# Sample tokens' experts gathered on four partition groups, dense experts on 512 tokens, an exponential decay, and new row quotas in a hybrid trunk layer

## The chip, the cores and the metric

One core of one Trainium2 chip runs the whole kernel. The metric is the device time of one execution in microseconds (us), the median of the runs shown. All data are fp32 in HBM; the large matmuls are done in passes of a high and a low half, as told below.

## The reference, cut to what matters

One layer is computed for 1024 prompt tokens and 32 sample tokens (next frames of a running stream), with D = 1024 channels. Three mixers (a gated convolution, an RG-LRU recurrence, an HGRN2 matrix recurrence) read one wide projection of x and are merged, a layer norm follows, then PEER: each token takes 8 heads x 16 = 128 single-neuron experts out of 16384.

```python
log_a = -LRU_C * r * softplus(-lam)            # RG-LRU, r a sigmoid
a = exp(log_a)
u = sqrt(-expm1(2.0 * log_a)) * (gi * xf)
h_t = a_t * h_{t-1} + u_t

def peer_block(xt, wq, keys, u_tab, v_tab):    # u_tab, v_tab: 16384 x 1024
    q = (xt @ wq).reshape(n, 8, 2, 128)
    s = einsum('nhpd,hpkd->nhpk', q, keys)
    sv, si = top_k(s, 16)                      # per half, then 16 of the 256 pair sums
    ...
    h = gelu(einsum('nd,nhkd->nhk', xt, u_tab[expert]))
    return einsum('nhk,nhkd->nd', g * h, v_tab[expert])
x = layer_norm(ALPHA * x + merged @ w_o)
x = layer_norm(ALPHA * x + peer(x))
```

## The kernel before

The tokens are taken in two halves: tokens 0 to 511 (four tiles of 128), then tokens 512 to 1023 together with the 32 sample tokens. Activations lie with channels on partitions. Every projection (`proj`, lines 327 to 340) has a 128-column weight tile in a high part wh (cast by ScalarE, L293) and a low part wl (the difference, made by VectorE at L297, or read back from HBM at L295), and eight k tiles of the input, again as high and low; it issues wh*xh (L334), wh*xl (L335) and wl*xh (L339), so 24 passes over all columns of the layout. A layout `Lay(n)` of over 512 columns is cut in two halves, and then each pass is two matmuls; one of 512 is one matmul.

PEER is done in two ways. **Gathered**: the first four tiles (the list `todo`, tokens 0 to 511). `gather` (L1214) loads, for each of a token's 128 experts, one row of `u` per partition by an indirect DMA that GpSimd issues (L1221; one "row" is a 128 x 1024 fp32 tile, 512 KB), multiplies and sums it on VectorE (L1230), then gelu, then the same with rows of `v` (L1238), and a layer norm. That is 256 rows per tile, 1024 in all, and they go through four row buffers (`big`, L878): GpSimd issues row k+4 when VectorE has used row k. **Dense**: tokens 512 to 1023 and the 32 sample tokens, 544 columns in two halves of 272. All 16384 experts' activations are computed as 128 projections of `ut` (`hidden`, L1091; 40 of them ahead of time, in the spread stage, kept in HBM as `hd`), multiplied by a weight matrix `gt` that is zero but for the chosen experts (L1134), cut in high and low (L1138, L1139), and multiplied by `vt` in 16 groups of 8 projections (L1146), added into eight accumulators (L1152). The weight matrix is made by `spread`, for 16 tokens at a time, from one-hot products (L1080, L1083, L1084) and staged in HBM as `gd`, 34 blocks of 16 tokens.

The rows of the gathered tiles are traced last in the program, and the framework's scheduler fixes each engine's order ahead of time; VectorE then runs its list strictly in order. `BESIDE` and `pacing` (L1256) hold the rows back: the program has marks (`cuts`) between stages, `BESIDE` says how many rows belong to each stage, and a row's VectorE instruction may not stand before an instruction at the matching share of that stage's matmuls. It is a lower bound only: nothing makes a row stand there if its data, its buffer or VectorE is not free. The seven stages and quotas of before are:

- the rest of the first half's top-k with mixer A of the second half: 92
- heads of the second half (`heads`): 125
- `outs` of the second half (mixer C's output, mixer B): 145
- output of mixer B, first norm, top-k of the second half: 94
- spread: 42
- dense groups 0 to 4, whose hidden projections were done ahead: 82
- dense groups 5 to 15, with 8 hidden and 8 `vt` projections each: 444 (spread over 97% of the matmuls, `EARLY`)

Mixer B (`mix_b`, L566) has the recurrence. Its decay a = exp(-2x) is formed from t = tanh(x) as 1 - 2t/(1+t), with a reciprocal on VectorE (L611) and, in the second half, two ScalarE affine steps (L608, L614); sqrt(t)/(1+t) scales the input (L604, L619, L620). It is called eight times in each half.

Of the kernel before, what the change touches and what calls it, by code (L numbers as in the profile page):

```python
# [57 lines left out]
BESIDE = 92, 125, 145, 94, 42, 82, 444  # L58
# [4 lines left out]
SPAN = 39  # L63
# [38 lines left out]
class K:  # L102
# [51 lines left out]
    def consts(self):  # L154
# [28 lines left out]
        pi = c.tile([128, 1], I32, name="pi")  # L183
        G.iota(pi, pattern=[[0, 1]], base=0, channel_multiplier=1)
        ct = ExitStack()
        t = ct.enter_context(self.tc.tile_pool(name="ct", bufs=1))
        ti = t.tile([128, 128], I32, name="ti")
# [9 lines left out]
        pb = c.tile([128, 1], I32, name="mpb")  # L197
        pf = c.tile([128, 2], F32, name="mpf")
# [73 lines left out]
        V.scalar_tensor_tensor(self.sp2, p, 4.0, u, op0=OP.mult, op1=OP.add)  # L272

# [292 lines left out]
    def mix_b(self, ct, out):  # L566
# [31 lines left out]
        t = tr  # L598
# [442 lines left out]
    def experts(self, ti, ijg):  # L1041
        V, B = self.nc.vector, self.bp
        ex = B.tile([128, 128], I32, name="ex", tag=f"ex{ti}")
        V.scalar_tensor_tensor(ex, ijg[:, 0:128], 128.0, ijg[:, 128:256], op0=OP.mult, op1=OP.add)  # L1044
        gw = B.tile([128, 128], F32, name="gw", tag=f"gw{ti}")
        V.tensor_copy(gw, ijg[:, 256:384])
        return ex, gw


    def spread(self, n, c0, ijg, H):  # L1050
# [4 lines left out]
        if H == 8:  # L1055
            for q in range(3):
                nc.tensor.transpose(pt[:, q * 128:(q + 1) * 128], ijg[:, q * 128:(q + 1) * 128], self.ident)
# [348 lines left out]
```

## Time and profile before

| | us |
|---|---|
| median of three runs | 4102.07 (4100.8 to 4104.7) |
| the profiled execution | 4098.35 |
| its span, first to last instruction | 4096.2 |
| PE busy / VectorE busy / ScalarE busy / GpSimd busy | 3799.3 / 3205.3 / 1471.7 / 1528.8 |

All later terms are made against the profiled execution: its time is 2.2 us more than its span, and 3.7 us below the median of the runs. The page gives the busy time of each engine, and busy shares in 40 slices; a matmul's end is modelled, so a busy PE is not PE at its peak rate. The rows below take the span apart by the stages above. The stretches meet where one stage's own lines end and the next one's begin: 1547 us is the end of the heads, 1846 the last mixer B product (L634), 2220 the last copy of a query (L940), 2661 the start of the dense groups, 2946 the first hidden projection of dense group 5, 4066 the last accumulation.

### The profile page before, as it was taken

What the parts mean: (1) busy time and instruction counts of PE and PEld (TensorE: products, weight loads), DVE (VectorE), ACT (ScalarE), POOL (GpSimd) and SP (SyncE); (2) the same over time, 40 slices, a digit from 0 to 9 for tenths busy, and PEclk for the clock granted to TensorE, in tenths of its full rate; (3) what the DMA queues carried; (4) which work ended last, traced back from release to release, by engine and by line L of the source; (5) the groups of instructions that cost most, each with busy time, mean ns of one, the idle gap of its engine ahead of it and who ended that gap; (6) DMA issues with size and microseconds to landing.
All of it is one profiled execution on the core that took longest, in us unless ns stands there. A gap on an engine that the chain in (4) does not pass through costs nothing.

```text
span 4096.2 us, 69951 instructions
## 1 busy us (share of the span) xinstructions
PE 3799.3 (93%) x26917; PEld 3543.6 (87%) x26917; DVE 3205.3 (78%) x6625; ACT 1471.7 (36%) x2352; POOL 1528.8 (37%) x1353
## 2 busy tenths in 40 slices
PE   9999999989899898999678998789999999999996
PEld 7888787789899887999668997689999999999996
DVE  6556438679997887885689999888788887878888
ACT  3333326433232223552233588722222222222222
POOL 0000000001345543343332688723356555555553
PEclk9999999999999998999889999899999999999998
DMA  5443455668998977998997887798899988888886
GB/s 189 144 144 132 154 190 177 217 236 299 366 341 295 319 277 246 339 321 334 366 343 283 279 277 241 214 337 317 287 321 325 324 315 306 315 311 315 316 317 233
DMA packets 377230, 1132.94 MB, mean 277 GB/s; under 512 B 34816, under 2 KB 109696, under 8 KB 374848
## 3 DMA queue, kind: packets, MB, share of 16 engines
q1 hardware_dynamic: 229440, 591.53, 40.9%
q0 software_dynamic: 147456, 536.94, 37.4%
q8 instruction: 212, 3.47, 0.3%
q14 instruction: 122, 1.00, 0.1%
HBM read 1000.48 MB, written 127.84 MB: 275 GB/s over the span
## 4 chain that ended last, share of the span: by engine, by line
PE 16%; DMA 11%; issue 9%; DVE 7%; POOL 6%; ACT 2%; SPq 0%; POOLq 0%; DVEq 0%; ACTq 0%
DMA row<-in_v,ex 7%; POOL row L1221 6%; PE z L339 5%; PE z L335 5%; PE z L334 4%; DVE x1g L1238 2%; PE t L1084 1%; DMA row<-in_u,ex 1%; DVE oa L1080 1%; DMA wl<-wl 1%; DVE wl L297 1%; ACT stg L1085 1%; DMA wraw<-in_wq 1%; DMA ge<-hd 1%; ACT ob L1074 0%
## 5 line engine op out<-in xcount | busy, mean ns | idle before, releaser
L334 PE MATMUL z<-h,wh 128*128 128x272 f32 (+5 forms) x4608 | 1315.4, 313 | 30.4 <-ACT wh L293 18.0
L335 PE MATMUL z<-l,wh 128*128 128x272 f32 (+5 forms) x4608 | 1303.7, 310 | 1.2 <-DVE l L370 1.2
L1221 POOL DMA_INDIRECT row<-in_u,ex x512 | 628.0, 1227 | 1510.0 <-DVE ex L1044 655.8
L293 ACT CAST wh<-wraw 128x1024 fp32r<-128x1024 f32 x568 | 596.3, 1050 | 1414.1 <-PE z L335 1130.7
L334 PEld LDWEIGHTS z<-h,wh 128*128 128x128 f32 x4608 | 878.0, 191 | 77.1 <-ACT wh L293 21.5
L1221 POOL DMA_INDIRECT row<-in_v,ex x512 | 665.4, 1300 | 688.5 <-DVE x1g L1238 469.4
L335 PEld LDWEIGHTS z<-l,wh 128*128 128x128 f32 x4608 | 878.8, 191 | 37.4 <-issue 2.7
L339 PE MATMUL z<-h,wl 128*128 128x272 f32 (+5 forms) x4608 | 744.6, 309 | 14.9 <-DMA wl<-wl 14.2
L1238 DVE SCALAR_TENSOR_TENSOR x1g<-row,hh,x1g 128x1024 f32<-128x1024 f32 x512 | 655.1, 1280 | 125.4 <-DMA row<-in_v,ex 121.7
L1230 DVE SCALAR_TENSOR_TENSOR row<-row,x1g 128x1024 f32<-128x1024 f32 x512 | 618.2, 1217 | 145.0 <-DMA row<-in_u,ex 144.4
L339 PEld LDWEIGHTS z<-h,wl 128*128 128x128 f32 x4608 | 649.9, 190 | 49.6 <-DMA wl<-wl 15.5
L297 DVE TENSOR_TENSOR wl<-wraw,wh 128x1024 fp32r<-128x1024 f32 x400 | 488.5, 1222 | 187.4 <-ACT wh L293 89.7
L335 PE MATMUL z<-dl,wh 128*128 128x272 f32 x2048 | 518.1, 292 | 29.6 <-DVE dl L1139 29.4
L334 PE MATMUL z<-dh,wh 128*128 128x272 f32 x2048 | 515.3, 293 | 10.2 <-ACT dh L1138 9.8
L335 PEld LDWEIGHTS z<-dl,wh 128*128 128x128 f32 x2048 | 386.3, 192 | 35.1 <-DVE dl L1139 35.1
L334 PEld LDWEIGHTS z<-dh,wh 128*128 128x128 f32 x2048 | 384.6, 192 | 14.3 <-ACT dh L1138 14.2
L339 PE MATMUL z<-dh,wl 128*128 128x272 f32 x2048 | 283.9, 292 | 23.8 <-DVE wl L297 23.8
L339 PEld LDWEIGHTS z<-dh,wl 128*128 128x128 f32 x2048 | 269.8, 192 | 25.4 <-DVE wl L297 25.4
L1138 ACT CAST dh<-w 128x544 fp32r<-128x544 f32 x128 | 82.4, 647 | 393.1 <-DVE w L1134 393.1
L1083 POOL TENSOR_SCALAR ob<-iota,tr 128x128 f32<-128x128 f32 x272 | 214.3, 801 | 22.1 <-PE t L1084 8.7
L1084 PE MATMUL t<-ob,oa 128*128 128x128 f32 x1088 | 167.8, 293 | 33.6 <-DVE oa L1080 15.9
L1084 PEld LDWEIGHTS t<-ob,oa 128*128 128x128 f32 x1088 | 147.8, 199 | 47.5 <-POOL ob L1083 15.1
(381 smaller groups left out, 4650.4 us busy)
## 6 DMA issues: line engine op xcount, KB each, us to landing
wl<-wl SPq DMA_DIRECT2D x304, 512.0 KB, 4.7
wraw<-in_w_in SPq DMA_DIRECT2D x192, 512.0 KB, 4.3
wraw<-in_vt SPq DMA_DIRECT2D x128, 512.0 KB, 6.4
wraw<-in_ut SPq DMA_DIRECT2D x128, 512.0 KB, 5.8
gd<-stg SPq DMA_DIRECT2D x34, 1024.0 KB, 6.3
gt<-gd SPq DMA_DIRECT2D x16, 2176.0 KB, 11.5
wraw<-in_wq SPq DMA_DIRECT2D x56, 512.0 KB, 6.9
wraw<-in_w_o SPq DMA_DIRECT2D x24, 512.0 KB, 6.2
```

Source lines behind the costliest of these rows:

```text
L293: nc.scalar.copy(wh, raw)
L297: nc.vector.tensor_sub(wl, raw, wh.bitcast(F32))
L334: mm(ps[:, :n], wh[:, k, :], xh[:, o:o + n], start=k == 0, stop=False)
L335: mm(ps[:, :n], wh[:, k, :], xl[:, o:o + n], start=False, stop=False)
L339: mm(ps[:, :n], wl[:, k, :], xh[:, o:o + n], start=False, stop=k == KT - 1)
L1080: V.tensor_scalar(oa, self.iota, tr[:, 0, t:t + 1], tr[:, 2, t:t + 1], op0=OP.is_equal, op1=OP.mult)
L1083: G.tensor_scalar(ob, self.iota, tr[:, 1, t:t + 1], None, op0=OP.is_equal)
L1084: nc.tensor.matmul(pw[:, s * 128:(s + 1) * 128], oa, ob, start=True, stop=True)
L1138: A.copy(hi, w)
L1221: nc.gpsimd.indirect_dma_start(out=u[:n], out_offset=None, in_=self.io[tab], in_offset=bass.IndirectOffsetOnAxis(ap=ex[:n, s:s + 1], axis=0))
L1230: V.scalar_tensor_tensor(u[:n], u[:n], 1.0, x1[:n], op0=OP.mult, op1=OP.mult, accum_out=hh[:n, s:s + 1])
L1238: V.scalar_tensor_tensor(x1[:n], u[:n], hh[:n, s:s + 1], x1[:n], op0=OP.mult, op1=OP.add)
```

## The change

- The sample's 32 tokens leave the dense part. Their 128 experts are kept as a 128 x 32 block, as `retrieve` already makes it (two heads' 32 experts on each of four groups of 32 partitions). The new `gather_packed` copies x1 of the 32 tokens four times onto the partitions, runs 32 rows of u and 32 rows of v on all 128 partitions, adds the four groups by three small DMAs and adds, and normalizes. It is traced ahead of the last gathered tile. That makes 1088 rows in place of 1024.
- The dense part has 512 tokens: one matmul of 512 columns per pass. `spread` loses its sample case: 32 blocks of 16 tokens instead of 34. The final tail has four tiles.
- `mix_b` computes a = exp(-2 sp2 (tr + 1)) by one ScalarE activation and takes 0.5 (1 + a) sqrt(t) as the input's scale: the reciprocal and the affine steps go.
- `BESIDE` becomes 92, 125, 195, 140, 35, 50, 451, and `SPAN` 37.

```diff
-BESIDE = 92, 125, 145, 94, 42, 82, 444
+BESIDE = 92, 125, 195, 140, 35, 50, 451
-SPAN = 39
+SPAN = 37
...
+        self.sp4 = e8("sp4")
+        V.tensor_scalar(self.sp4, self.sp2, -2.0, None, op0=OP.mult)
...
-        t = tr
+        t, a = sq, tr
...
         A.activation(t[:, :N], tr[:, :N], AF.Tanh, scale=self.sp2[:, ct:ct + 1], bias=self.sp2[:, ct:ct + 1])
+        A.activation(a[:, :N], tr[:, :N], AF.Exp, scale=self.sp4[:, ct:ct + 1], bias=self.sp4[:, ct:ct + 1])
         A.activation(sq[:, :N], t[:, :N], AF.Sqrt)
-        rc, a = self.et(), t
-        if b and FA > 1:
-            A.activation(rc[:, :N], t[:, :N], AF.Identity, bias=self.one)
-        else:
-            V.tensor_scalar(rc[:, :N], t[:, :N], 1.0, None, op0=OP.add)
-        V.reciprocal(rc[:, :N], rc[:, :N])
-        V.tensor_mul(a[:, :N], t[:, :N], rc[:, :N])
-        if b and FA:
-            A.activation(a[:, :N], a[:, :N], AF.Identity, scale=-2.0, bias=self.one)
-        else:
-            V.tensor_scalar(a[:, :N], a[:, :N], -2.0, 1.0, op0=OP.mult, op1=OP.add)
...
-        V.tensor_mul(v[:, :N], v[:, :N], sq[:, :N])
-        V.tensor_mul(v[:, :N], v[:, :N], rc[:, :N])
+        V.scalar_tensor_tensor(sq[:, :N], a[:, :N], 1.0, sq[:, :N], op0=OP.add, op1=OP.mult)
+        V.scalar_tensor_tensor(v[:, :N], v[:, :N], 0.5, sq[:, :N], op0=OP.mult, op1=OP.mult)
...
+            if H < 8:
+                self.packed = (t, *self.experts(t[0], ijg))
             yield
-            yield from self.spread(t[3], t[2], ijg, H)
+            if H == 8:
+                yield from self.spread(t[2], ijg)
...
+    def gather_packed(self, t, ex, gw):
+        nc, (_, g0, _, n) = self.nc, t
+        V = nc.vector
+        x1 = self.x1g(128)
+        for q in range(4):
+            nc.sync.dma_start(x1[n * q:n * q + n], self.x1d[g0:g0 + n, :])
+        def mid():
+            V.tensor_scalar(x1[:n], x1[:n], ALPHA, None, op0=OP.mult)
+            for q in range(1, 4):
+                V.memset(x1[n * q:n * q + n], 0.0)
+        self.retrieved(x1, 128, ex, gw, 32, x1, mid)
+        for q in range(1, 4):
+            u = self.big()
+            nc.sync.dma_start(u[:n], x1[n * q:n * q + n])
+            V.tensor_add(x1[:n], x1[:n], u[:n])
+        self.finished(x1, g0, n)
...
-    k.gd = k.dp.tile([16, 128, 34, 128], F32, name="gd")
+    k.gd = k.dp.tile([16, 128, 32, 128], F32, name="gd")
-        dt = k.tiles(1)[4 - ND:]
+        dt = k.tiles(1)[4 - ND:4]
-            c0, L = (4 - ND) * 128, Lay(ND * 128 + SMP)
+            c0, L = (4 - ND) * 128, Lay(ND * 128)
         for t in todo:
+            if t is todo[-1]:
+                k.gather_packed(*k.packed)
-            k.gather(t[0], t[1], t[3], t[4], t[5])
+            k.gather(t[1], t[3], t[4], t[5])
```

`retrieved` and `rows`, which both gathers call, hold the loops of the old `gather` unchanged but for the number of rows.

## Rows read from the trace of the kernel before

**Rows 1.** The profile's page: span, busy time by engine, and the DMA engines' busy tenths in 40 slices of the span.

```profile
span 4096.2 us, 69951 instructions
PE 3799.3 (93%) x26917; PEld 3543.6 (87%) x26917; DVE 3205.3 (78%) x6625; ACT 1471.7 (36%) x2352; POOL 1528.8 (37%) x1353
...
DMA  5443455668998977998997887798899988888886
```

**Rows 2.** The busy times by stretch, all instructions: stretch, its length, busy us (and instructions) of PE, PEld, DVE, ACT, POOL, then granted clock, DMA share, GB/s.

```profile
700.00:800.00 100.00, 96.73 (x404) 75.10 (x403) 72.33 (x93) 52.12 (x67) 0.00 (x0) 1.00 0.58 201
...
1547.00:1846.00 299.00, 289.95 (x2147) 273.68 (x2148) 238.48 (x363) 151.56 (x224) 113.94 (x93) 0.97 0.85 307
...
2220.00:2661.00 441.00, 389.63 (x2971) 374.64 (x2971) 421.49 (x1237) 313.87 (x615) 320.08 (x354) 0.96 0.80 253
2661.00:2946.00 285.00, 260.30 (x1971) 255.53 (x1970) 225.12 (x350) 69.93 (x86) 86.58 (x80) 0.96 0.89 317
2946.00:4066.00 1120.00, 1080.65 (x8492) 1074.01 (x8490) 928.44 (x1185) 294.72 (x445) 608.90 (x442) 0.99 0.89 314
4066.00:4096.20 30.20, 0.00 (x0) 0.00 (x0) 25.43 (x53) 8.92 (x16) 0.00 (x0) 0.53 0.27 99
```

**Rows 3.** The same view for line 1221 alone, the row issues on GpSimd: stretch, its length, POOL busy (and issues), granted clock, DMA share, GB/s. The last row is the same view for line 1238 (rows of v used by VectorE), for one stretch of 100 us.

```profile
970.00:1150.00 180.00, 62.69 (x59) 1.00 0.96 360
1150.00:1547.00 397.00, 189.03 (x152) 0.94 0.86 303
1547.00:1846.00 299.00, 113.94 (x93) 0.97 0.85 307
1846.00:2220.00 374.00, 126.51 (x117) 0.88 0.91 338
2220.00:2661.00 441.00, 105.77 (x82) 0.96 0.80 253
2661.00:2946.00 285.00, 86.58 (x80) 0.96 0.89 317
2946.00:4066.00 1120.00, 608.90 (x442) 0.99 0.89 314
...
3100.00:3200.00 100.00, 55.09 (x43) 1.00 0.94 333
```

**Rows 4.** The timeline of PE inside dense group 12: start us, duration, line, operation. One projection of 48 matmuls of 272 columns lies between the first and the last row.

```profile
3760.62 0.29 PE L334 MATMUL z<-h,wh 128*128 128x272 f32 x1
...
3764.63 2.16 PE L339 MATMUL z<-h,wl 128*128 128x272 f32 x16
3766.63 0.29 PE L334 MATMUL z<-h,wh 128*128 128x272 f32 x1
```

**Rows 5.** The timeline of PE in the first half, where the layout has 512 columns: 16 matmuls start between these two rows.

```profile
212.49 0.39 PE L334 MATMUL z<-h,wh 128*128 128x512 f32 x1
...
216.21 2.02 PE L339 MATMUL z<-h,wl 128*128 128x512 f32 x8
```

**Rows 6.** VectorE's groups of instructions in the stretch 2946 to 4066 us: line, operation, tiles, shape, count | busy us, mean ns | idle us ahead of them and who ended it.

```profile
L1238 DVE SCALAR_TENSOR_TENSOR x1g<-row,hh,x1g 128x1024 f32<-128x1024 f32 x255 | 326.8, 1282 | 89.7 <-DMA row<-in_v,ex 87.0
L1230 DVE SCALAR_TENSOR_TENSOR row<-row,x1g 128x1024 f32<-128x1024 f32 x190 | 228.8, 1221 | 68.4 <-DMA row<-in_u,ex 67.9
...
L1152 DVE TENSOR_TENSOR acc<-acc,z 128x272 f32<-128x272 f32 x178 | 70.2, 430 | 28.1 <-PE z L339 27.8
L1139 DVE TENSOR_TENSOR dl<-w,dh 128x544 fp32r<-128x544 f32 x88 | 63.2, 718 | 0.0
...
L1230 DVE DVE_READ_ACCUMULATOR row<-row,x1g 128x1 f32 x190 | 15.4, 81 | 0.0
```

**Rows 7.** VectorE's waits in the same stretch: who waited for whom, us in total, times, longest.

```profile
DVE x1g L1238 <- DMA row<-in_v,ex: 87.0, 68, 6.1
DVE row L1230 <- DMA row<-in_u,ex: 67.9, 50, 6.9
```

**Rows 8.** PE's longest waits in the same stretch.

```profile
PE z L339 <- DVE wl L297: 23.8, 7, 4.4
```

**Rows 9.** Row DMAs in the same stretch: issues, and median us from issue to landing.

```profile
row<-in_v,ex POOLq DMA_INDIRECT x256, 6.8
row<-in_u,ex POOLq DMA_INDIRECT x186, 6.5
```

**Rows 10.** Groups of instructions of mixer B, whole span: two of VectorE in the second half, and ScalarE's table loads ahead of the square root (L604) and of the gelu (L589).

```profile
L611 DVE RECIPROCAL e<-e 128x548 f32<-128x548 f32 x8 | 28.6, 3575 | 1.1 <-ACT e L608 1.1
...
L612 DVE TENSOR_TENSOR e<-e 128x548 f32<-128x548 f32 x8 | 5.8, 723 | 0.0
...
L604 ACT ACT_TABLE_LOAD x16 | 20.5, 1283 | 0.3
L589 ACT ACT_TABLE_LOAD x14 | 18.0, 1283 | 0.2
```

**Rows 11.** VectorE's costliest group in the spread stage, 2220 to 2661 us.

```profile
L1080 DVE TENSOR_SCALAR oa<-iota,tr 128x128 f32<-128x128 f32 x544 | 170.7, 393 | 0.0
```

**Rows 12.** Two VectorE groups on 512 columns in the first half, one with an operand in PSUM (L854) and one without (L634).

```profile
L854 DVE SCALAR_TENSOR_TENSOR m<-e,z 128x512 f32<-128x512 f32 x8 | 5.5, 685 | 22.4 <-PE z L339 22.4
...
L634 DVE TENSOR_TENSOR e<-e 128x512 f32<-128x512 f32 x8 | 5.5, 682 | 0.0
```

**Rows 13.** The timeline of GpSimd where the third gathered tile ends and the fourth begins: in brackets the idle time ahead of the issue and who ended it.

```profile
3423.56 1.68 POOL L1221 DMA_INDIRECT row<-in_u,ex  x1 [8.06 <-DVE x1g L874]
```

More of the change, by code (lines that the diff above doesn't have):

```diff
@@ L196, in consts @@
         tb = t.tile([128, 128], I32, name="mtb")
-        pb = c.tile([128, 1], I32, name="mpb")
-        pf = c.tile([128, 2], F32, name="mpf")
+        pb = t.tile([128, 1], I32, name="mpb")
+        pf = t.tile([128, 2], F32, name="mpf")
         tf = t.tile([128, 128], F32, name="mtf")
@@ L1042, in experts, with spread @@
         V, B = self.nc.vector, self.bp
[L1043 to L1046, printed above, removed]
+        m = ijg.shape[1] // 3
+        ex = B.tile([128, m], I32, name="ex", tag=f"ex{ti}")
+        V.scalar_tensor_tensor(ex, ijg[:, 0:m], 128.0, ijg[:, m:2 * m], op0=OP.mult, op1=OP.add)
+        gw = B.tile([128, m], F32, name="gw", tag=f"gw{ti}")
+        V.tensor_copy(gw, ijg[:, 2 * m:3 * m])
         return ex, gw
-    def spread(self, n, c0, ijg, H):
+    def spread(self, c0, ijg):
         nc = self.nc
@@ L1211, in paced @@
         return self.tc.issue_after(self.pace[min(k, len(self.pace) - 1)])
-    def gather(self, ti, g0, n, ex, gw):
-        nc = self.nc
-        V, A, B = nc.vector, nc.scalar, self.gp
-        hh = B.tile([128, 128], F32, name="hh", tag="hh", bufs=2)
-        def row(tab, s):
-            u = self.big()
-            nc.gpsimd.indirect_dma_start(out=u[:n], out_offset=None, in_=self.io[tab],
-                                         in_offset=bass.IndirectOffsetOnAxis(ap=ex[:n, s:s + 1], axis=0))
-            return u
-        x1 = self.gp.tile([128, D], F32, name="x1g", tag="x1g", bufs=X1G)
-        nc.sync.dma_start(x1[:n], self.x1d[g0:g0 + n, :])
-        for s in range(128):
-            u = row("u", s)
-            with self.paced():
-                V.scalar_tensor_tensor(u[:n], u[:n], 1.0, x1[:n], op0=OP.mult, op1=OP.mult,
-                                       accum_out=hh[:n, s:s + 1])
-        A.activation(hh[:n], hh[:n], AF.Gelu)
-        V.tensor_mul(hh[:n], hh[:n], gw[:n])
-        V.tensor_scalar(x1[:n], x1[:n], ALPHA, None, op0=OP.mult)
-        for s in range(128):
-            u = row("v", s)
-            with self.paced():
-                V.scalar_tensor_tensor(x1[:n], u[:n], hh[:n, s:s + 1], x1[:n], op0=OP.mult, op1=OP.add)
-        self.ln(x1, n, self.eps[:, 1:2], self.lnvec("ln2_g"), self.lnvec("ln2_b"), x1, "g")
-        nc.sync.dma_start(self.io["y"][g0:g0 + n, :], x1[:n])
@@ new lines, in rows, with retrieved @@
+    def rows(self, tab, n, ex, m, f):
+        for s in range(m):
+            u = self.big()
+            self.nc.gpsimd.indirect_dma_start(out=u[:n], out_offset=None, in_=self.io[tab],
+                                              in_offset=bass.IndirectOffsetOnAxis(ap=ex[:n, s:s + 1], axis=0))
+            with self.paced():
+                f(u, s)
+    def retrieved(self, x1, n, ex, gw, m, acc, mid):
+        V = self.nc.vector
+        hh = self.gp.tile([128, 128], F32, name="hh", tag="hh", bufs=2)
+        self.rows("u", n, ex, m, lambda u, s: V.scalar_tensor_tensor(
+            u[:n], u[:n], 1.0, x1[:n], op0=OP.mult, op1=OP.mult, accum_out=hh[:n, s:s + 1]))
+        self.nc.scalar.activation(hh[:n, :m], hh[:n, :m], AF.Gelu)
+        V.tensor_mul(hh[:n, :m], hh[:n, :m], gw[:n])
+        mid()
+        self.rows("v", n, ex, m, lambda u, s: V.scalar_tensor_tensor(
+            acc[:n], u[:n], hh[:n, s:s + 1], acc[:n], op0=OP.mult, op1=OP.add))
```

30 lines of the change are left out of this document (17 added, 13 removed).

## The prediction

> **What bounds the kernel now.** I read the page first: PE is busy for 93% of the span, VectorE for 78%, and from the middle of the first half on the DMA engines stand at eight or nine tenths in nearly every slice [rows 1]. An average over stages with different limits says little, so I read the busy times by stretch next [rows 2], and the row issues in the same stretches [rows 3]. Two things come out. In the last stage, 2946 to 4066 us (dense groups 5 to 15, 1120 us, over a quarter of the span), PE is busy for 1081 us. But VectorE is hardly less tied up: 928 us busy [rows 2] and another 155 us standing still in front of a row that has not landed [rows 7], 1083 us of 1120. So PE and the rows end there together, and a change that relieves PE alone is worth only what the rows let it be worth. The second thing is where the rows run. The quotas ask for 92 + 125 + 145 = 362 rows by 1846 us, 456 by 2220, 498 by 2661; issued were 304, 421 and 503 (sums of the counts in [rows 3]; an issue is up to four rows ahead of VectorE). So between 1547 and 2661 us the quota did not hold the rows back; they ran as fast as buffers, DMA and VectorE's order let them, and caught up only at the end of the spread. After that they follow the plan: 583 issued by 2946, where 580 were due.
>
> **PE in the dense part.** A projection of 544 columns is 48 matmuls of 272, and takes 6.01 us (3760.62 to 3766.63) [rows 4], 125 ns a matmul. With 512 columns 16 matmuls start in 216.21 - 212.49 = 3.72 us [rows 5], 232.5 ns each, 24 of them 5.58 us. The change is worth 0.43 us per projection: 17 us over the 40 `vt` projections of dense groups 0 to 4, 76 us over the 176 of groups 5 to 15, and 17 us over the 40 ahead of time in the spread. PE's floor for the last stage is 1120 - 76 = 1044 us, waits as now. PE's own largest wait there, 23.8 us on wl [rows 8], is VectorE's lateness, so it does not shrink by itself.
>
> **How many rows the dense part gets.** The new quotas put 587 of 1088 rows ahead of the dense part, 88 more than the 499 that VectorE had done by 2661 us. I don't believe that they get there, since the stretches where the quotas rise (145 to 195, 94 to 140) are those in which they did not bind. What can make rows faster there: mixer B loses a reciprocal of 3.58 us and a product of 0.72 us for each of eight channel tiles [rows 10], 34 us of VectorE's 238 in 1547 to 1846 [rows 2]. If this stretch came to the pace of the one ahead of it (152 in 397 us, 2.61 us a row [rows 3]) it would have 114 rows instead of 93, 21 more. From 1846 to 2220 us the DMA moved 338 GB/s; the most in any row here is 360, and 22 GB/s for 374 us are 15 rows of 0.524 MB. In the spread VectorE loses 32 of 544 one-hot products of 0.31 us (170.7 / 544 [rows 11]), 10 us, 8 rows at 1.28 us. So 0 to 44 more; I take 20, near the first term, the one with a cause in the diff. Then 1088 - 519 = 569 rows are left for the dense part (545 to 589), against 525 before (80 + 445).
>
> **The stages, one by one.** *First half*: VectorE loses a reciprocal, a product and two affine steps per channel tile, ScalarE gains the exponential; PE is busy for 97 of 100 us there [rows 2], and covers it: 0 (-3 to 0). *1547 to 2220*: PE covers the mixer (290 of 299 us); 20 more rows of DMA share the queues with weights: 0 (-5 to +10). *Spread*: VectorE is busy 421 of 441 us [rows 2], so its time counts: 10 us of one-hot products, plus small copies of the sample; PE's 17 us are mostly behind it. I take -12 (-25 to 0; the low end is two steps of 34 and PE's share, the high end that new rows eat it). *2661 to 2946*: the old plan held the rows to 82; now a backlog of about 68 stands behind the new quota of 50. Bytes: 317 GB/s x 285 us = 90.3 MB, of which 80 rows are 41.9; the other 48.4 become 47.1 by the narrower hd and gd. At 338 GB/s, the rate of 1846 to 2220, 270 us carry 91.3 MB, 84 rows. I take 270 us, -15 (-17, PE's floor, to +5). That leaves 569 - 84 = 485 rows for the last stage, where 442 were issued before.
>
> *The last stage* has four bounds for 485 rows. PE: 1044 us. DMA: now 314 GB/s x 1120 us = 351.7 MB, 231.7 of them rows; 120 + 485 x 0.524 = 374 MB, at 338 GB/s 1107 us (at the 360 of the best row 1039, at today's 314 1191). The row loop: four buffers, each gone for a landing of 6.8 us [rows 9], 1.28 us of VectorE [rows 6] and the issue; the fullest 100 us hold 43 rows [rows 3], at which 485 take 1128. VectorE: rows cost 571.0 us busy (326.8 + 228.8 + 15.4) [rows 6] and 154.9 of waiting [rows 7], 1.63 us each for 445; everything else is 928 - 571 = 357. Of this, the accumulation falls from 2 x 0.430 us to one of about 0.685 on 512 columns, and the products with the gate and the low halves from 0.718 to about 0.682 each [rows 6, 12], 17 us together; the packed tile's last adds and norm bring about 12. So 352 + 485 x 1.63 = 1143 us with waits as now, 974 with none. I take 1110, between the DMA term and these, so -10 (-76 to +71, by 1044 and 1191). The packed tile adds one more tile boundary; the last one held the issues for 8.06 us behind the norm [rows 13], and more rows queue behind it on GpSimd, which is within that range. *End*: 30.2 us after the last accumulation, VectorE 25 of them [rows 2]; one tile of five is gone: -3 (-5 to 0).
>
> Sum: 0 + 0 - 12 - 15 - 10 - 3 = -40 us, so 4098.35 - 40 = 4058 as profiled, and with the 3.7 us by which the median lies above that execution, 4062. The gain of PE, 93 us in the dense part, is mostly spent on 64 more rows that have nowhere else to go. The forecast's own spread is 4030 to 4094.
>
> **The rivals.** (A) *The rows keep up and PE sets the end.* Then the last stage takes 1044 us: -12 - 15 - 76 - 3 = -106, 3992, as a median 3996. For it: VectorE needs only 974 us without waits, and 374 MB in 1044 us is 358 GB/s, which one stretch of 180 us reached [rows 3]. Against it: that stretch is a sixth as long, and 485 rows would need 2.15 us each, where the fullest 100 us show 2.33. (B) *The row loop outlasts PE, slower than before.* Rows that VectorE has not done when PE ends run alone behind it. At the pace at which the old plan asked for rows (0.97 x 1120 / 444 = 2.45 us) 485 take 1187 us: +67 - 30 = +37, 4135, as a median 4139; at today's mean of 2.53 us 1229, and 4181. It decides from 2.37 us a row on, where the stage takes 1150. For it: the waits of 155 us and the DMA share of 0.89 show little slack, and more bytes make landings later. Against it: today's pace is set by the quota, and while PE's list was behind, rows were seen at 2.33. (C) *No change*: the stage takes 1140 to 1155, PE's gain and the 64 rows cancel: 4094 to 4110. (D) *The exponential costs ScalarE time.* Tanh now runs behind the gelu's table load with no load of its own, and the square root has one (16 and 14 loads of 1.283 us) [rows 10]. If the exponential needs a further load, ScalarE has 16 x 1.283 = 20.5 us more; it is busy 152 of 299 us in that stretch [rows 2], so it should be hidden; uncovered it would add 20 to the forecast, 4082. The Trainium skill, page "ScalarE: Activation LUTs", section "Table sets: the hidden batching unit", puts exp and tanh in one set and gelu and sqrt in others, by which that load would come; the rows of before can't show it.
>
> **How the numbers follow.** Forecast 0.45, A 0.20, B 0.17, C 0.13, D 0.05. About 0.2%, 8 us, is what a measurement of this kernel can tell from no change. Faster by more: forecast, A and D, 0.70; same: C, 0.13; slower: B, 0.17. The range leaves out the better half of A and the worse half of B, some 0.18: 3990 to 4130.
>
> **What would show it.** Right: 24 matmuls 232 ns apart in the dense part; about 520 row issues by the start of the dense part, whatever the quotas say (587 would be wrong, and point to A); in the last stage VectorE busy or waiting on rows nearly all the time, DMA at 0.93 or more, PE with new gaps that end on wl or dl, perhaps a lower granted clock; few or no rows after the last dense matmul. B would show as row products alone on VectorE, with PE idle, for tens of us at the end. Wrong would also be a spread stage longer than 441 us, or a stretch 1547 to 2220 that grows by more than 10.

## The result, and the profile after

The changed kernel takes 4132.5 us (median of 4 runs, 4128.5 to 4133.6) against 4103.1 for the kernel before on the same chip: ratio 1.0078, 95% interval 1.0060 to 1.0096, slower (the two medians alone give 1.0072). The forecast was 4062, faster; the time lies 2.5 us beyond the upper end of the range, near where rival B had put it (4139). The profiled execution took 4132.6 us, its span 4130.8.

The page after, which answers to [rows 1]: span, busy time of PE and VectorE, busy tenths of the DMA engines.

```profile
span 4130.8 us, 57366 instructions
PE 3699.7 (90%) x20700; PEld 3150.2 (76%) x20700; DVE 3192.3 (77%) x6519; ACT 1465.6 (35%) x2200; POOL 1606.3 (39%) x1401
...
DMA  5443455678988878998998887889999988999977
```

PE is busy for 100 us less, as wanted, and the span grew by 35. Where it went is seen in the busy times by stretch, cut at the same events as [rows 2]; the columns are those there, and POOL's count is that of the rows issued. The lines are dense groups 0 to 4, groups 5 to 15, the rows behind the last matmul, and the end:

```profile
2653.00:2950.00 297.00, 258.85 (x960) 194.19 (x961) 243.26 (x372) 65.76 (x80) 130.51 (x107) 0.86 0.92 327
2950.00:3975.00 1025.00, 999.72 (x4253) 800.14 (x4253) 865.42 (x1056) 290.73 (x361) 540.54 (x400) 0.99 0.90 320
3975.00:4121.60 146.60, 0.64 (x6) 0.39 (x4) 105.51 (x108) 6.93 (x12) 85.93 (x67) 0.51 0.81 269
4121.60:4130.80 9.20, 0.00 (x0) 0.00 (x0) 4.87 (x7) 0.29 (x1) 0.00 (x0) 0.50 0.14 58
```

The second line stands where [rows 2] had 1120 us (1118 from the first projection of group 5 to the end of the last accumulation): groups 5 to 15 now take 1025, with PE busy for 1000 of them. The third line is new: 147 us in which PE does next to nothing (0.64 us), with a granted clock of 0.51, and VectorE and the DMA engines go on. Before, the last row was done 3.5 us behind the last accumulation; now 70 rows are. The sum of the differences is the result: group 5 begins at 2950 instead of 2946 (+4), groups 5 to 15 are 93 us shorter, the rows alone are 143 longer (147 for 3.5), and the end is 19 shorter, since the dense part's last norm now lies beside the rows: +35.

VectorE in that third stretch, from its timeline: start, duration, line, operation, in brackets the idle time ahead and who ended it. Row after row, each behind its own DMA.

```profile
4040.12 1.28 DVE L1222 SCALAR_TENSOR_TENSOR x1g<-row,hh,x1g 128x1024 f32<-128x1024 f32 x1 [0.65 <-DMA row<-in_v,ex]
4042.09 1.28 DVE L1222 SCALAR_TENSOR_TENSOR x1g<-row,hh,x1g 128x1024 f32<-128x1024 f32 x1 [0.69 <-DMA row<-in_v,ex]
4043.91 2.60 DVE L1222 SCALAR_TENSOR_TENSOR x1g<-row,hh,x1g 128x1024 f32<-128x1024 f32 x2 [0.53 <-DMA row<-in_v,ex]
```

VectorE's waits from 2950 to 3975 us, which answer to [rows 7] (155 us there, 123.5 here): even with fewer rows in the stage, rows were late 92 times.

```profile
DVE x1g L1222 <- DMA row<-in_v,ex: 67.5, 46, 6.2
DVE row L1217 <- DMA row<-in_u,ex: 56.0, 46, 6.1
DVE acc L1142 <- PE z L341: 28.3, 24, 2.8
```

Two sizes that the prediction took from elsewhere, in VectorE's groups of the same stretch (compare [rows 6, 12]), and PE's timeline inside a projection (compare [rows 4, 5]): 3402.14 - 3399.81 = 2.33 us for ten matmuls, 233 ns each.

```profile
L1142 DVE TENSOR_TENSOR acc<-acc,z 128x512 f32<-128x512 f32 x89 | 60.8, 683 | 28.5 <-PE z L341 28.3
L1129 DVE TENSOR_TENSOR dl<-w,dh 128x512 fp32r<-128x512 f32 x88 | 60.2, 684 | 0.0
```

```profile
3399.81 0.40 PE L337 MATMUL z<-dl,wh 128*128 128x512 f32 x1
...
3402.14 0.40 PE L337 MATMUL z<-dl,wh 128*128 128x512 f32 x1
```

### The profile page after: what moved, and what is told of

The parts are those of the page before. It is cut to its first block, busy times and chain, and to the rows that moved or that the text cites. A ratio compares the mean times of both kernels' runs of the same rounds, so it can differ in the third digit from the quotient of the medians.

```text
span 4130.8 us, 57366 instructions
## 1 busy us (share of the span) xinstructions
PE 3699.7 (90%) x20700; PEld 3150.2 (76%) x20700; DVE 3192.3 (77%) x6519; ACT 1465.6 (35%) x2200; POOL 1606.3 (39%) x1401
## 4 chain that ended last, share of the span: by engine, by line
PE 19%; issue 10%; DMA 9%; POOL 7%; DVE 5%; ACT 1%; POOLq 0%; SPq 0%; DVEq 0%; ACTq 0%
POOL row L1208 7%; PE z L341 6%; DMA row<-in_v,ex 6%; PE z L337 6%; PE z L336 5%; DMA row<-in_u,ex 2%; PE t L1071 2%; DVE x1g L1222 1%; DVE oa L1067 1%; PE t L938 0%; DMA wl<-wl 0%; DVE wl L299 0%; POOL ob L1070 0%; DVE row L1217 0%; DMA keys<-in_keys 0%
## 5 line engine op out<-in xcount | busy, mean ns | idle before, releaser
L336 PE MATMUL z<-h,wh 128*128 128x512 f32 (+4 forms) x3584 | 1197.2, 350 | 37.0 <-ACT wh L295 20.6
L337 PE MATMUL z<-l,wh 128*128 128x512 f32 (+4 forms) x3584 | 1187.8, 347 | 1.2 <-DVE l L372 1.2
L336 PEld LDWEIGHTS z<-h,wh 128*128 128x128 f32 x3584 | 686.4, 192 | 124.6 <-ACT wh L295 23.4
L337 PEld LDWEIGHTS z<-l,wh 128*128 128x128 f32 x3584 | 686.7, 192 | 82.1 <-issue 2.9
L341 PE MATMUL z<-h,wl 128*128 128x512 f32 (+4 forms) x3584 | 721.0, 345 | 11.3 <-DMA wl<-wl 9.4
L336 PE MATMUL z<-dh,wh 128*128 128x512 f32 x1024 | 411.0, 410 | 44.8 <-ACT dh L1128 44.4
L337 PE MATMUL z<-dl,wh 128*128 128x512 f32 x1024 | 415.7, 412 | 30.7 <-DVE dl L1129 30.7
L341 PE MATMUL z<-dh,wl 128*128 128x512 f32 x1024 | 271.8, 409 | 9.6 <-DVE wl L299 9.6
L336 PEld LDWEIGHTS z<-dh,wh 128*128 128x128 f32 x1024 | 197.7, 195 | 100.6 <-ACT dh L1128 54.0
L337 PEld LDWEIGHTS z<-dl,wh 128*128 128x128 f32 x1024 | 198.3, 195 | 94.1 <-DVE dl L1129 49.1
```

Of the source, the lines that this page charges most:

```text
L336: mm(ps[:, :n], wh[:, k, :], xh[:, o:o + n], start=k == 0, stop=False)
L337: mm(ps[:, :n], wh[:, k, :], xl[:, o:o + n], start=False, stop=False)
L341: mm(ps[:, :n], wl[:, k, :], xh[:, o:o + n], start=False, stop=k == KT - 1)
```

## The experiments

Four theories were weighed. R: the round trip of the four row buffers (issue, landing, product, free again) sets 2.5 us a row beside the dense work. Q: the new quotas cost the time. V: VectorE has no time left for more rows. M: the DMA engines are full. Later expectations name two more: S, the order that the scheduler draws up ahead of time holds the last stage to 400 rows, and O, the order written by hand holds it itself. For every run the table gives groups 5 to 15 (from the first projection of group 5 to the last accumulation), the rows that VectorE began in it (counted from its two row lines), and the rows left alone behind the last accumulation. "By hand" is explained at its run.

| kernel | rows before group 5 | groups 5 to 15, us | rows in it | us a row | alone: rows, us | time, us |
|---|---|---|---|---|---|---|
| before | 578 | 1118 | 445 | 2.51 | 1, 4 | 4103 |
| changed | 619 | 1025 | 399 | 2.57 | 70, 147 | 4132 |
| old quotas | 579 | 1015 | 398 | 2.55 | 111, 225 | 4160 |
| no sample rows | 622 | 1011 | 402 | 2.51 | none | 4003 |
| half products | 637 | 989 | 400 | 2.47 | 51, 98 | 4005 |
| six buffers | 636 | 993 | 401 | 2.48 | 51, 93 | 4070 |
| four, by hand | 617 | 1166 | 465 | 2.51 | 6, 13 | 4148 |
| six, by hand | 635 | 1044 | 448 | 2.33 | 5, 12 | 4052 |
| seven, by hand | 636 | 1035 | 447 | 2.31 | 5, 13 | 4048 |
| half rows | 637 | 987 | 451 | 2.19 | none | 3856 |
| before + six buffers | 579 | 1062 | 445 | 2.39 | none | 4040 |
| six, by hand, more rows early | 668 | 1019 | 415 | 2.46 | 5, 12 | 4066 |
| before + decay | 578 | 1119 | 445 | 2.52 | 1, 4 | 4087 |
| before + decay + six buffers | 579 | 1061 | 445 | 2.38 | none | 4026 |
| six, by hand, half the bytes | 636 | 1014 | 447 | 2.27 | 5, 12 | 4011 |
| six, by hand, low halves free | 635 | 1060 | 448 | 2.37 | 5, 12 | 4054 |

**Old quotas.**

```diff
-BESIDE = 92, 125, 195, 140, 35, 50, 451
+BESIDE = 92, 125, 145, 94, 42, 82, 508
```

> The changed kernel with the quotas of before (92, 125, 145, 94, 42, 82) and all other rows, 508, in the last stage. Theory R (the row loop ends the kernel, and the raised quotas of the middle stages did nothing, because the rows were not held there): about as many rows done when the dense part starts as the 512 of the changed kernel, 495 to 510, fewer by dense group 5, and 4130 to 4160 us. Theory Q (the new quotas themselves cost the time, by putting rows where they delay weights): 4100 us or less.

Measured 4159.5 us, ratio to before 1.0148 (1.0119 to 1.0177): 27 us worse than the changed kernel, so Q falls; the new quotas help. Up to group 5 this run has 40 rows fewer and comes there 40 us earlier, and these rows then run alone, where they cost 78 us (225 for 147): a row ahead of group 5 cost about 1.0 us here, one behind the last accumulation 1.9. Dense groups 0 to 4, groups 5 to 15, and the rows alone, by stretch as above:

```profile
2644.00:2910.00 266.00, 245.26 (x961) 187.74 (x962) 218.35 (x314) 67.34 (x82) 99.22 (x80) 0.92 0.89 315
2910.00:3926.00 1016.00, 997.09 (x4256) 800.17 (x4254) 863.00 (x1094) 292.13 (x361) 530.94 (x399) 0.99 0.90 322
3926.00:4150.00 224.00, 0.00 (x0) 0.00 (x0) 157.25 (x148) 6.93 (x12) 135.96 (x108) 0.51 0.80 270
```

It settles a point of the prediction besides. The last quota is 508 here instead of 451, and groups 5 to 15 still take 398 rows: what holds the rows in that stage is not the quota.

**No sample rows.** The 64 rows of the packed tile and its three adds are left out and the last quota is 387; everything else stays.

```diff
-        self.retrieved(x1, 128, ex, gw, 32, x1, mid)
-        for q in range(1, 4):
...
+        mid()
```

> The changed kernel without the 64 rows of the sample: their gathered products and the three adds are left out, so the sample's rows of y lack PEER; the norm and the store stay, the last quota is 387. Theory R: matmuls end where they do in the changed kernel (3976 us into the span), 0 to 20 rows are left then, and the whole takes 3990 to 4020 us; the 64 rows cost 110 to 140 us. Theory Q: over 4080 us.

Measured 4003.2 us, ratio 0.9766 (0.9742 to 0.9789). The rest of the change (narrower dense part, decay, quotas) is worth 99 us against before, and the 64 rows cost 129, 2.0 us each: the price of a row that runs alone, as if nothing lay beside it.

**Six row buffers.** Two more in a pool that opens with the dense part, used by every third row from row 540 on.

```diff
+        late = getattr(self, "npaced", 0) >= LATER
+        pool, bufs = (self.gx, 2) if late and self.nbig % 3 == 0 else (self.gp, 4)
-        return self.gp.tile([128, D], F32, name="row", tag="row", bufs=4)
+        return pool.tile([128, D], F32, name="row", tag="row", bufs=bufs)
```

> The changed kernel with two more row buffers from the dense part on (six instead of four; from the 540th row on every third tile is one of the two). Theory R, by buffers (four buffers' turn sets 2.5 us a row): VectorE's waits on rows (123 us in the last stage, 40 behind it) mostly go, the last stage takes in 40 to 70 rows more, 4020 to 4080 us. Theory V (VectorE has no time left beside the dense work, so more buffers change nothing): 4115 to 4140 us. Theory M (DMA engines are full): landings get longer with more in flight, 4115 to 4140 us, DMA share as now.

Measured 4069.7 us, ratio 0.9929 (0.9904 to 0.9953). Buffers are worth 63 us, faster than both kernels: group 5 begins 18 us later with 17 rows more done, groups 5 to 15 are 31 us shorter, and the rows alone 53 us shorter. The time is the one that R gave, but not in the way it said: groups 5 to 15 still take only 401 rows. Their stretch, the rows alone behind it, and VectorE's waits in the first:

```profile
2968.00:3962.00 994.00, 988.17 (x4256) 798.16 (x4255) 869.03 (x1041) 297.53 (x361) 534.72 (x401) 1.00 0.91 331
3962.00:4055.00 93.00, 0.46 (x5) 0.22 (x3) 80.67 (x88) 6.93 (x12) 60.81 (x47) 0.51 0.87 310
```

```profile
DVE acc L1146 <- PE z L342: 74.8, 53, 4.3
...
DVE row L1221 <- DMA row<-in_u,ex: 8.1, 3, 4.1
...
DVE x1g L1226 <- DMA row<-in_v,ex: 0.2, 1, 0.2
```

VectorE now waits 75 us for PE and 8 for rows, so late rows no longer held it to 401; it takes instructions in the order drawn up ahead of time, and that order has 400 rows in this stage (2.27 a projection) and 51 behind the last accumulation. Alone, six buffers do a row in 1.83 us, four in 2.09.

**Half products.** The row products go over 512 of 1024 columns; the DMAs stay whole.

```diff
-            u[:n], u[:n], 1.0, x1[:n], ...
+            u[:n, :512], u[:n, :512], 1.0, x1[:n, :512], ...
```

> The changed kernel with the rows' products on VectorE over half of the 1024 columns, all row DMAs as they are: the gathered tokens' result lacks half of each product. Theory V (VectorE's time): a row takes 0.6 us less of VectorE, 280 us in the dense part, all rows fit beside the matmuls, 3990 to 4020 us. Theory R, by buffers: the turn of a buffer shortens by 0.6 of about 10 us, some 0.16 us a row, 30 to 45 rows are still left after the last matmul, 4050 to 4090 us. Theory M: 4110 or more.

Measured 4005.2 us (one run), inside V's range and below R's. VectorE's time counts, 127 us (41 of them up to group 5, 36 in groups 5 to 15, 49 in the rows alone), but not by being full, as V has it: in groups 5 to 15 it was busy for 671 of 990 us and did the same 400 rows as with whole products. V by itself is out, since 51 rows are still left behind the last accumulation. A shorter product frees its buffer earlier, and where rows run alone the gain is the one that R foresaw (1.92 us a row for 2.09); R left out the 41 us up to group 5 and the 36 in the stage.

**The order by hand, six buffers and four.** The rows are traced inside the dense loop. From group 5 on, behind each of the 176 projections come 448 / 176 row products, and the next low half or sum of the dense part is tied behind them, so that about 450 rows must be done before the last sum. Once with six buffers, once with the changed kernel's four.

```diff
+    def dues(self, jc, i):
+        p = jc * 16 + i + 1 - AHEAD * 2
+        if p > 0:
+            self.due(min(len(self.pace) + p * LAST // 176, LAST + len(self.pace)))
...
+                    with self.behind(jc):
                         for v, p in L.each(ps):
                             V.tensor_add(v(acc[d]), v(acc[d]), p)
+                    self.dues(jc, 8 + d)
```

> The kernel with six row buffers, and the order of VectorE in groups 5 to 15 written by hand: behind each of the 176 projections 448/176 row products, and the next lo or sum of the dense part only behind them. Up to 637 rows lie ahead of group 5 as before. So about 445 rows must be multiplied before the last sum, where the four runs before this one had 398 to 402 whatever their buffers, quotas or products. Theory S (the order drawn up ahead of time, and nothing on the chip, holds the last stage to 400 rows): groups 5 to 15 stay at TensorE's 994 us (six buffers) or up to 1005, under 10 rows are left alone, median 3985 to 4010 us. Theory M (the 16 DMA engines are full: they were 0.91 busy at 331 GB/s in that stage with six buffers): 445 rows of 0.524 MB and 118 MB of weights and gates are 351 MB, at 331 GB/s 1060 us, so the stage grows by what the rows behind it shrink, median 4045 to 4070 us.

> The same order written by hand, with the four row buffers of the changed kernel. Ahead of group 5 it has 620 rows, in groups 5 to 15 about 462. Theory R (four buffers carry no more than one row per 2.5 us beside the dense work, 2.1 us alone): VectorE now waits for rows inside the stage, and TensorE behind it: 462 rows at 2.1 to 2.5 us are 970 to 1155 us, taken near the upper end as in the kernel before (2.53), 1120 us, median 4090 to 4110 us, little better than the changed kernel's 4132. Theory S (only the order): 1010 to 1030 us, median 3990 to 4020 us. Theory M: 360 MB at the 320 GB/s of the changed kernel's stage are 1125 us, the same as R; the run with six buffers tells those two apart.

Six buffers: 4052.5 us, ratio 0.9880 (0.9850 to 0.9911). Four: 4147.9, ratio 1.0109 (1.0081 to 1.0136). Groups 5 to 15 with four, by stretch, then VectorE's waits there and PE's:

```profile
2957.00:4124.00 1167.00, 1027.61 (x4256) 814.32 (x4255) 949.75 (x1124) 289.14 (x361) 626.13 (x466) 0.93 0.88 311
```

```profile
DVE x1g L1259 <- DMA row<-in_v,ex: 99.2, 77, 6.4
DVE row L1254 <- DMA row<-in_u,ex: 69.7, 48, 6.0
```

```profile
PE z L337 <- DVE dl L1134: 123.4, 29, 12.9
```

The 70 rows are back inside the stage, and it is 141 us longer: VectorE waits 169 us for rows and PE 123 us for VectorE. So with four buffers the order hardly matters: 471 rows in the stage and behind it take 1179 us, 469 took 1172 in the changed kernel. The 465 rows inside come at 2.51 us, as in the kernel before; that the second digit agrees may be chance. R holds for four buffers, though its time (4090 to 4110) was too low: the pace of 2.51 gives 1166 us, not 1120. With six, all else the same, the stage is 122 us shorter, so four buffers are what held it and not the DMA engines, which move 338 GB/s here for 311. But it is still 50 us above PE's 994, in M's range and not in S's (3985 to 4010): the planned order was not the only thing that kept the rows out. The stage, and what PE waits for in it:

```profile
2973.00:4018.00 1045.00, 1004.51 (x4258) 804.79 (x4256) 925.03 (x1087) 294.39 (x361) 616.05 (x448) 0.98 0.92 338
```

```profile
PE z L338 <- DVE dl L1138: 38.9, 16, 11.2
```

**Half rows.** Each row gathers 512 of 1024 columns; four buffers, the planned order, and products as in the run with half products.

```diff
-indirect_dma_start(out=u[:n], ..., in_=self.io[tab], ...
+indirect_dma_start(out=u[:n, 0:512], ..., in_=self.io[tab].rearrange("r (t c) -> (r t) c", t=2), ...
```

> The changed kernel with rows of half the length: each row gathers 512 of 1024 columns (2 KB), and the products go over these alone; the other half of the PEER term is left out. Beside the run with half products and whole rows only the bytes differ. That run took 4005 us with 400 rows in groups 5 to 15. Theory S with the planned bytes as what limits the order: all 1088 rows are multiplied before the last sum, and the kernel ends with TensorE, 3920 to 3980 us. If the order were held by the number of rows (one issue of GpSimd each) and not by their bytes, 400 rows again in that stage and 51 left, alone at the 1.3 us of an issue: some 3975 to 4000 us.

Measured 3856.4 us (one run), 149 less than with half products and whole rows: more than foreseen, since the stages ahead gain too (group 5 begins 63 us earlier). The last rows end 20 us before the last sum, so the order does follow the planned bytes: the same 1088 rows at half the bytes all come in. Its stretch, and the rows' landing in it (median us behind the issues; 6.8 and 7.1 in the run by hand with six buffers):

```profile
2846.00:3833.00 987.00, 986.01 (x4253) 796.72 (x4252) 704.91 (x1095) 295.82 (x361) 527.75 (x447) 1.00 0.75 241
```

```profile
row<-in_v,ex POOLq DMA_INDIRECT x287, 4.0
row<-in_u,ex POOLq DMA_INDIRECT x160, 4.1
```

**Seven buffers by hand, six buffers in the kernel before, and more rows early.** The first is the run by hand with a third extra buffer; the second is the kernel before with the diff of the six buffers and nothing else; the third is the run by hand with six buffers and `BESIDE = 110, 150, ...`, `LAST = 405`.

> The run with six buffers and the order by hand once more, with seven row buffers from the dense part on. With six, groups 5 to 15 took 1045 us for 448 rows, TensorE 1005 of them busy, the DMA engines 0.92 at 338 GB/s. Theory M (DMA engines full): the seventh buffer only makes each row wait longer among more packets; the stage stays within 1035 to 1050 us at 0.92 to 0.93, median 4040 to 4060 us. Theory R (the buffers' round trip): seven rows in flight instead of six take the stage to its TensorE floor, 995 to 1010 us, median 4005 to 4020 us.

> The kernel before (544 tokens in the dense part, 1024 rows) with six row buffers from the dense part on, and nothing else changed. Its order has 583 rows ahead of group 5 and all of the rest before the last sum, which ends with TensorE. Theory R: with four buffers groups 5 to 15 waited on rows inside; with six the stage falls from 1118 to TensorE's 1055 to 1085 us, as the changed kernel's fell to its floor, median 4040 to 4075 us: then the dense part of 512 tokens is worth next to nothing beside the same buffers (4070 with the order drawn up, 4052 by hand). Theory M: 441 rows, 118 MB of weights and gates at 331 to 338 GB/s are 1033 to 1047 us, under TensorE's floor, so the same. If VectorE (928 us busy of 1120) or something else held that stage, it stays at 1100 to 1120 us, 4085 to 4105 us.

> The run with six buffers and the order by hand, with the quotas of the first two stages raised from 92 and 125 to 110 and 150, so that the order has 555 rows before the first dense group (528 there) and 668 before group 5 (635), and 405 rows by hand in groups 5 to 15 (448). Theory M: 43 rows fewer are 22 MB fewer among 353, at 338 GB/s 67 us, so that stage ends at TensorE's 990 to 1005 us; if the first half carries the rows at no cost, median 4000 to 4020 us. If the first half pays for them as the last stage does, 2.0 to 2.5 us a row, 4035 to 4060 us, no gain.

Seven: 4048.1 us, ratio 0.9874 (0.9841 to 0.9908), the DMA share again 0.92, at 339 GB/s: the seventh buffer changed next to nothing, as M has it. VectorE waits only 11 us for rows there, though, so what holds the stage is no longer a late row. Nor is it shown that the DMA engines are full: in dense groups 0 to 4 of the same run they move 345 GB/s. Groups 0 to 4, then 5 to 15:

```profile
2695.00:2979.00 284.00, 251.71 (x960) 188.93 (x961) 243.09 (x373) 67.40 (x82) 136.29 (x106) 0.90 0.94 345
```

```profile
2979.00:4014.00 1035.00, 1001.76 (x4255) 802.81 (x4254) 923.43 (x1085) 295.28 (x361) 600.15 (x445) 0.98 0.92 339
```

The kernel before with six buffers: 4040.2 us, ratio 0.9846 (0.9812 to 0.9879), less than the changed kernel with six, seven, or the order by hand (4048 to 4070; the 8 us to the run with seven are within the two intervals). Its last stage is all PE:

```profile
2948.00:4012.00 1064.00, 1063.91 (x8491) 1063.54 (x8490) 930.88 (x1190) 306.85 (x446) 593.06 (x441) 1.00 0.91 330
```

The same 445 rows took 1118 us with four buffers: R and M both foresaw a stage at PE's floor, and VectorE's time did not hold it. So once the buffers are there, 544 dense tokens with 1024 rows beat 512 with 1088, clear of noise when both have the new decay (4026, below, against 4048): PE gets 70 us shorter in this stage (1064 to 994), and the 64 rows cost more than that.

More rows early: 4065.9 us, ratio 0.9909 (0.9876 to 0.9942). The last stage did fall, to 1019 us with 415 rows, but group 5 began 48 us later (3022 instead of 2973) for 33 more rows. The earlier stages pay for these rows as well, 1.5 us each: of the 48 us, 20 are there at the last mixer B product, 29 at the last product with the keys, 45 at the first dense group. Neither of the two stages that got them was a free place.

**The decay alone, and the best of both.** The kernel before with mixer B's exponential only; and that with six buffers.

```diff
+            A.activation(a[:, :N], tr[:, :N], AF.Exp, scale=self.sp4[:, ct:ct + 1], bias=self.sp4[:, ct:ct + 1])
-            V.reciprocal(rc[:, :N], rc[:, :N])
-            V.tensor_mul(a[:, :N], t[:, :N], rc[:, :N])
...
```

> The kernel before with the exponential decay of mixer B alone (544 columns, sample among the dense tokens, old quotas). Its order of VectorE holds as many rows at every stage edge as the kernel before (499 at the first dense group, 583 at group 5, 1023 by the last sum). All theories: no difference, 4085 to 4105 us against the kernel before, since mixer B's stage ends with TensorE and the rows' order is the same. If the reciprocals taken away (16 of 3.58 us on VectorE) did lie on the path, up to 57 us less.

> The two parts that gained alone, together: the kernel before with 544 dense tokens and 1024 rows, mixer B's exponential decay (4087 alone, 0.9968) and six row buffers from the dense part on (4040 alone, 0.9846). TensorE is busy in all of groups 5 to 15 with six buffers (1064 us of 1064), so nothing more can be had there; the decay's gain lies ahead of the dense part. If both add up: 4025 to 4035 us, ratio 0.980 to 0.983. If they share one wait: 4038 to 4045 us.

The decay alone: 4086.9 us, ratio 0.9968 (0.9952 to 0.9984), a small gain where none was expected; the first dense group begins at 2656 instead of 2668, with the same 499 rows. In the one trace the last mixer B product ends 9 us earlier (1836 for 1846), the last product with the keys 6 earlier, and the spread adds the rest; behind the first dense group some 5 of the 12 are lost again, so the trace's own gain is 7 and the medians' 11. Both together: 4025.9 us, ratio 0.9814 (0.9796 to 0.9832), the fastest kernel of this study that does the whole computation, and 107 us ahead of the changed one. The two gains add up.

**What holds the order by hand at 1045 us.** Two runs on the one with six buffers: the same order with rows of half the bytes, each product going over the 512 gathered columns twice so that VectorE's 1.28 us stay (1279 ns measured); and the low halves set free of the rows.

```diff
-                with self.behind(jc):
-                    V.tensor_sub(lo, w, hi.bitcast(F32))
+                V.tensor_sub(lo, w, hi.bitcast(F32))
```

> The run with six buffers and the order by hand (448 rows in groups 5 to 15, 4052 us, that stage 1045 us where TensorE's floor is 987 to 994), with rows of half the bytes: each gathers 512 of 1024 columns, and the product goes over these twice, so that VectorE's instructions keep their 1024 columns; the other half of the PEER term is left out. Only the bytes differ. Theory M (bytes hold that stage): 990 to 1000 us, as in the run with half rows in the planned order. Theory O (the order by hand holds it: lo stands behind rows that it needn't wait for): 1030 to 1045 us again. In both the stages ahead of group 5 are shorter, 2850 us up to there instead of 2973.

> The same run with whole rows, six buffers and 448 rows by hand, but only the sums of the dense part stand behind the rows; lo (the low half that the output projections wait for) may be put ahead of them. TensorE waited for lo 16 times, 38.9 us in total, and for nothing else. Theory O: these waits go, groups 5 to 15 take 995 to 1010 us, median 4005 to 4025 us. Theory M: the wait moves to the weights' low halves or to the sums, 1030 to 1050 us, median 4040 to 4060 us.

Half the bytes: 4010.5 us (one run), the stage 1014 us for 447 rows, between the forecasts of M and O. The stage, and PE's waits on the low halves, which fell from 38.9 to 13.5 us:

```profile
2965.00:3978.00 1013.00, 994.93 (x4250) 799.68 (x4248) 922.21 (x1084) 294.07 (x360) 637.32 (x445) 0.99 0.70 232
```

```profile
PE z L338 <- DVE dl L1138: 13.5, 9, 2.8
```

The start of group 5 did not come at 2850 but at 2964. By the first dense group the run has done 588 rows, as many as the run with half rows in the planned order, but each takes 1.22 to 1.28 us of VectorE instead of 0.69 to 0.75, and the last product with the keys and the spread end 28 and 117 us later. Low halves free: 4054.0 us, ratio 0.9881 (0.9853 to 0.9908), the stage 1060; PE waits less on the low halves (20.9 us) and more on the sums (38.0):

```profile
PE z L1190 <- DVE acc L1152: 29.1, 5, 18.6
PE z L338 <- DVE dl L1137: 20.9, 5, 11.2
PE z L337 <- DVE acc L1152: 8.9, 1, 8.9
```

That is the wait that M foresaw for that run, with a stage 10 us above M's range. So of the 50 us above PE's floor some 30 go with the bytes, and 20 stay with bytes halved. Whether these 20 belong to the order by hand was not settled: freeing the low halves didn't bring them.

## Why the prediction was wrong

**What held.** PE: 233 ns a matmul (232.5 taken), and a stage that PE can end in 987 to 994 us, below the floor of 1044, since that floor carried the waits along (without waits the kernel before, with six buffers, takes 1064; 76 less is 988). The 512-column VectorE operations: 683 and 684 ns (685 and 682 taken). Of the 17 us taken off VectorE's other work the sums and the low halves gave 12.4 by the lines above, the gate's product 2.9 more. Rows by the start of the dense part: 512, where I took 519 and the quotas ask for 587; the higher quotas indeed did not bind. First half and mixers, taken as 0: the heads' own lines end at 1572 us for 1574 (the stretches of [rows 2] meet earlier, at 1547), and the last product with the keys ends at 2218 for 2220; in between the last mixer B product came 9 us earlier (1837 for 1846), and the next stretch, with ten rows more done at its end, gave most of it back. Spread: the first dense matmul at 2653 instead of 2668, -15 for the -12 taken. That agreement is in part luck: the -12 was for fewer one-hot products, and the decay alone, with none of them gone, brings that matmul 12 us forward; the changed kernel has 13 rows more to carry by then.

Of the signs named, 24 matmuls 232 ns apart and about 520 issues by the dense part came (515); a DMA share of 0.93 or more (0.90) and few or no rows after the last dense matmul (70) did not, and B's sign did.

**Rival D's load came and doesn't show in the time.** ScalarE's groups over the whole span, which answer to [rows 10]: the exponential (L606) has 14 loads, the square root (L607) 16 as before.

```profile
L607 ACT ACT_TABLE_LOAD x16 | 20.5, 1283 | 0.1
L591 ACT ACT_TABLE_LOAD x14 | 18.0, 1283 | 0.2
L606 ACT ACT_TABLE_LOAD x14 | 18.0, 1283 | 0.3
```

These 18 us are more than made up for: with the decay alone the kernel is faster. The Trainium skill, page "ScalarE: Activation LUTs", section "Table sets: the hidden batching unit", by which a change of set needs a load, agrees with the count: in mixer B most tanh run without a load behind the gelu's, and 14 of the 16 exponentials behind them have one. Its figure of about 2.7 us for a load is not what one costs here: the trace has 1.283, and in mixer B the activations ahead of it and behind it mostly lie within 20 ns.

**The step that failed** is the last stage's term. I priced 485 rows at 1110 us, 2.29 a row, "between the DMA term and these", and set rival B aside because "today's pace is set by the quota" and 100 us had shown 43 rows, 2.33 each. Both reasons fell. With the last quota at 508 the rows came no faster (398 in 1015 us; what held them at 400 there was the order drawn up ahead), and with the order by hand, where VectorE had to take them, four buffers gave 2.51 us a row over 1166 us. That is the mean of the kernel before, 1118 / 445, and the kernel before does the same 445 rows in 1062 us with two buffers more and the same quota: its pace was the row loop's own and had no slack, and the fullest 100 us were a peak. The rows that I left for the stage were 485 and came to 469 (399 inside at 2.57, 70 behind at 2.09): at 2.5 us each 1172, and the two stretches make 1025 + 147 = 1172, where I had 1110 for 485.

The mechanism was rival B's, rows alone behind PE, and its sum, 485 rows at 2.45 or 2.53, was the right one, with 16 rows too many. That its 4139 lies 7 us from the measured time is in part luck: 1187 us for the stage was 15 too many, the -30 for the rest came to -16, and the 2.45 was taken for the pace of the plan, which set nothing. The range closed at 4130, below both of B's figures, so it left out more of B than its worse half. B's bound stood in the trace in a form that I misread: 155 us of waiting on rows in [rows 7] already said that the rows, not the quota, were late. (C's stage of 1140 to 1155 us gives 4092 to 4107 by the same terms, not 4094 to 4110; nothing hangs on it.)

**A smaller miss** is dense groups 0 to 4. I took 270 us for 84 rows; it was 297 for 107. The run with the old quotas has 266 us for 80 rows, so the price of a stage with so many rows was right, and more rows came in than I took: these 23 came out of the last stage. That was a gain: the 27 rows more than with the old quotas cost 31 us here, 1.1 each. The end, -19 for -3, is no gain of its own: the norm of the dense tiles went under the rows left alone.

**The mechanism, then.** Moving 32 sample tokens from the dense part to rows takes some 70 us off PE in groups 5 to 15 and adds 64 rows of 2.0 to 2.5 us, 129 by the run without them. In no stage that was tried is a row free, though the price differs, from about 1.0 us ahead of group 5 to 2.0 behind the last matmul: with four buffers the loop is tied to a buffer's round trip, a landing of 6.8 us [rows 9] among it, and with six in part to the bytes; some 20 us of that last stage stay open. PE's relief only changes who is last, from both together [rows 2, 7] to the rows by themselves.

## What to carry to other kernels

When two resources end a stage together, a change that trades work from one to the other is priced at the other's full mean rate, taken over the whole stage; a peak of 100 us is no proof of slack, and waits on a transfer, on an engine that is otherwise busy nearly all the time, are a sign that there is none. Before trading, add the buffers that the slower loop lacks: two more gave the unchanged kernel 61 us here, where the trade cost 29. An order drawn up ahead of time hides which limit holds; writing it by hand for one stage helps to tell the two apart (with four buffers it settled the matter, with six 20 us stayed open).

## What the runs showed of the hardware

A gathered row of 128 x 4 KB landed in a median of 6.5 to 7.6 us beside the dense weights, in groups 5 to 15 of the kernel before and of the runs by hand with four, six and seven buffers; in the run with half rows, 128 x 2 KB landed in 4.0 to 4.1. The weights' own 512 KB took 6.3 to 6.5 us in the run by hand with six buffers and 3.8 to 4.2 in the one with half rows: with half the bytes in each row both came sooner (the two runs differ in order, buffers and products too). Groups 5 to 15 stood at 338 and 339 GB/s with six and with seven buffers by hand, at a DMA share of 0.92. That is not the most that the DMA engines moved: groups 0 to 4 of the run with seven moved 345 at 0.94, and [rows 3] has 360 at 0.96.

The granted clock stood at 1.00 where PE never waited (the kernel before with six buffers) and at 0.93 where it waited 123 us for low halves (four buffers by hand), 0.51 behind the last matmul. The same 4256 matmuls kept PE busy for 988 us in the stage with six buffers and for 1028 in the one with four by hand, so that 139 us of standing still went with 40 us of slower matmuls.
